# A new order for the opening of a hybrid decoder step, and other buffers for the gate's weights

## The chip, the core and the metric

The kernel runs on one core of one Trainium2 chip. A core has five engines, each with a queue of its own that it works through in order: TensorE (PE in the profile; its loads of weights are PEld) multiplies matrices and writes to PSUM; VectorE (DVE), ScalarE (ACT) and GpSimd (POOL) work element by element on SBUF, VectorE and ScalarE on PSUM too; SyncE (SP) issues DMAs here. ScalarE's queue issues DMAs as well. Engines wait for one another, and for DMAs, by semaphores.

The metric is the time of one execution on the device in microseconds (us). A profiled execution gives the trace, a time for each instruction; its span runs from the first instruction to the last.

## The reference: what is computed

One layer works on 1024 rows of a prompt and on 64 rows of samples (8 sequences of 8), each row 1024 wide, all in float32:

```python
mod = jax.nn.silu(c) @ w_ada + b_ada               # c: 1 + 8 rows, w_ada: 1024 x 3072
shift, scale, gate = jnp.split(mod, 3, axis=-1)
h = rmsnorm(x, norm_g) * (1 + scale[:, None]) + shift[:, None]
proj = h @ w_in                                    # the one large projection
u_pool, z_pool, z_ssm, xbc, dt_raw, g_raw = jnp.split(proj, SPLITS, axis=-1)
...                                                # pooling branch p, state-space branch s
gates = jax.nn.sigmoid(g_raw)
m = gates[..., :D_MODEL] * p + gates[..., D_MODEL:] * s
x = x + gate[:, None] * (m @ w_o)
```

The change lies in the first three lines and the first columns of the fourth. The gate, the last third of `mod`, isn't needed before the last line; it is computed early and put by in HBM.

## The kernel before

All 1088 rows (1024 and 64) are kept side by side as columns, so that a matrix of activations is eight tiles (k = 0 to 7) of 128 features by 1088 columns. The columns are cut into three blocks b: 0 is 256 wide, 1 is 384, 2 is 448 (384 of the prompt and the 64 samples).

**The opening** is the function `first()`. It loads x, normalises it, transposes it, computes shift and scale from `w_ada`, forms h, and does the first products with `w_in`. What it does is a set of small steps, and the order in which all engines take them is a list of words written out by hand, `ORDER1`. The steps are emitted in the order of the list, and `in_line` ties the instructions of each engine into that order (L219, the calls at the start and the end of `first`); so an engine never passes a step that waits. A word is a step's name, a number or two, and, where there is a choice, the engine: `.V` VectorE, `.A` ScalarE, `.G` GpSimd. The words that matter here:

- `sq i`: the sum of squares of 128 rows of x (VectorE L671, ScalarE L673); i = 8 is the samples. `root g`, `unit g`, `spread g`, `rsb g`: for block g the root (ScalarE), its reciprocal on a diagonal (VectorE or ScalarE), that spread over the partitions by PE (L696), and its copy to SBUF (ScalarE L705).
- `turn g.k`: PE transposes block g of x, features k, into a PSUM bank (L713): two 128-row tiles for block 0, three for 1, three and the samples for 2. `out g.k` scales it on VectorE and so frees the bank (L718). There are seven banks for all steps; a word takes the one that was freed longest ago.
- `silu`, `tab`, `cturn`, `sct`: c through SiLU, a table load for ScalarE, c transposed, and copied.
- `ada p.k`: PE multiplies c with rows k and k + 1 of part p of `w_ada` (L763). `mr`, `end`, `md` finish part p (ScalarE, PE, VectorE L778 and L781). Part p gives shift and scale for features 2p and 2p + 1.
- `h b.k`: ScalarE writes h rounded to the matmul's type (L794, L796). `ta`, `t b.k`: the same unrounded on ScalarE or VectorE (L803, L805, L812); `l b.k`: their difference, the low part (L658, a step with two inputs in SBUF). Each float32 product is made of three: high by high, low by high, high by low.
- `hi`, `lo`: the same split of a raw weight tile (L829, L658). `pr b.k`: PE adds feature tile k of block b to the first two output tiles (L844); `sg b.t` is their sigmoid and store (L857). `dt i`, `dto i`: the dt columns (L868).
- `gt k`: PE multiplies c with rows k and k + 1 of the gate's third of `w_ada` (L882); `ge` adds the bias and stores the gate.
- `ca`, `cb`, `cc`, `ce`, `s n h k`, `s n l k`: sums and differences of h for a product by seven half-sized products (Strassen's scheme), and their high and low parts (VectorE L658, ScalarE L940). S2 and S3 are two sets of four each. `wh n`, `wl n`: the same for the weights. `m n.s`: one half of the n-th of the seven products, twelve matmuls (PE L989). `u`, `z` put the products together.
- `warm n`: n matmuls whose result is not used.

**Loads.** SP's loads stand in a list `waiting`; behind each word, those at its head go out whose conditions have been said. The order is: x 0 to 4, the eight rows of part 0 of `w_ada`, two weight tiles, x 5 to 7, part 1, part 2, two more weight tiles, part 3, the dt columns, two column tiles `col`, six small loads, and the first four gate rows (`gate_load`, L606). The samples' x goes out on ScalarE's queue, behind four small loads of biases and gains. A completion semaphore is used again by a later DMA, so that an issue can wait for the landing of an earlier one.

**Buffers.** x lies in two large tiles, `xbig`, with the tag Y, of which there are two buffers; S2 and S3 later take the same two. Gate rows take three buffers with the tag R and the one with the tag sq; rows 4 to 7 take them again, and `gt` itself issues these loads, when rows k and k + 1 have been multiplied (end of `gt`).

**Behind the opening** come the units, pairs of column tiles of `w_in`, each seven half-sized products with all preparation of weights beside them (`pair`, L413 on PE, L151 and L154 for the split of weights). A planner of the language sets the order of their instructions, and PE goes from one to the next.

Of the kernel before, what the change touches and what calls it, by code (L numbers as in the profile page):

```python
# [46 lines left out]
def tile_pool_ssd_step(  # L47
# [34 lines left out]
    hs = open_("hs", 3)  # L82
# [3 lines left out]
    tfp = right.__enter__()  # L86
# [23 lines left out]
    load = nc.sync.dma_start  # L110
    store_ = nc.scalar.dma_start
# [70 lines left out]
    def x_load(i, start=None):
        n = P if i < 8 else NS
        xt = R([P, D]) if i == 8 else xbig[i // 4][:, i % 4, :D]
        (start or load)(xt[:n], x_prompt[0, i * P:(i + 1) * P, :] if i < 8 else x_sample.rearrange("b t d -> (b t) d"))
        xr[i] = (xt, n)
# [9 lines left out]
    def ada_load(part, k):  # L196
        a, b = PARTS[part]
        w = (b - a) * P
        if part == 0:
            if k == 0:  # L200
                wtile[0] = Y4(hp, F32)
            t = wtile[0][:, k // 2, k % 2 * 512:k % 2 * 512 + 2 * w]
        else:
            if k % 2 == 0:
                wtile[part, k // 2] = G((P, D))
            t = wtile[part, k // 2][:, k % 2 * 512:k % 2 * 512 + 2 * w]
        wraw[part, k] = t.rearrange("p (s c) -> p s c", s=2)
        load(wraw[part, k], w_ada[0, k * P:(k + 1) * P, 0:2 * D].rearrange("p (s c) -> p s c", s=2)[:, :, a * P:b * P])
# [49 lines left out]
    def dram(name, shape, dt=F32):  # L258
        return dr.tile(list(shape), dt, tag=name, name=name)
# [339 lines left out]


    gate_d = dram("gate_d", [NB + 1, D])
    gw, gp2 = {}, []

    def gate_load(k):
        gw[k] = hs.tile([P, D], F32, tag="sq", name=nm("gk"), bufs=1) if k % 4 == 3 else R((P, D))
        load(gw[k], w_ada[0, k * P:(k + 1) * P, 2 * D:])  # L606

    def gate_bias():
        bg = tfp.tile([P, 256], F32, tag="bg", name="bg", bufs=1)
        nc.gpsimd.memset(bg, 0.0)  # L610
        for j in range(4):
            load(bg[32 * j:32 * j + NB + 1], b_ada[0, 2 * D + 256 * j:2 * D + 256 * j + 256].partition_broadcast(NB + 1))
        return bg

    ORDER1 = """
        warm6 sq0.A silu sq1.V turn0.0 turn0.6 turn0.7 turn0.5 turn0.2 cturn tab sq2.V vturn warm2 sct root0
        sq8.V sq3.A turn0.1 warm8 unit0.V sq4.A vt spread0 root1 rsb0.A ada0.0 unit1.V ada0.2 out0.0 out0.1
        spread1 out0.2 turn1.2 out0.5 rsb1.A turn1.5 out0.6 turn1.1 out1.2 turn1.0 turn1.3 out1.1 turn1.4
        out1.3 ada0.4 out1.0 hi0.0 ada0.6 out1.5 mr0 turn0.4 hi1.0 lo0.0.V end0 turn0.3 md0 turn1.6 lo1.0.G
        turn1.7 sq5.A warm10 out0.3 out0.7 out1.4 h0.0 sq6.V h0.1 h1.0 turn2.4 t0.0.V sq7.A turn2.1 t1.0.V  # L620
        turn2.2 l0.0.V turn2.0 h1.1 l1.0.V ada1.0 t0.1.V root2 warm2 unit2.A l0.1.V ada1.2 t1.1.V warm4
        out1.6 l1.1.V ada1.4 out1.7 spread2 out0.4 pr1.0 rsb2.A out2.1 ada1.6 out2.2 mr1 turn2.7 ta2.1.A
        out2.4 end1 pr1.1 out2.0 t2.1 ta2.0.A ada2.0 md1 h2.1 ada2.2 ada2.4 t2.0 h0.3 turn2.6 h0.2 ta2.2.V
        ada2.6 h2.0 t2.2 turn2.3 mr2 hi0.1 turn2.5 l2.0.V end2 h1.3 l2.1.G out2.3 warm4 h2.2 out2.6 t1.3.A
        l2.2.V ada3.0 h1.2 l1.3.V pr2.0 hi1.1 lo0.1.G out2.7 t1.2.A md2 pr2.1 ta2.3.A l1.2.V h0.5 ta2.4.V
        ada3.2 h1.5 t2.3 ada3.4 t0.2.A ada3.6 t2.4 h2.3 pr0.0 mr3 l0.2.V h2.4 l2.3.V pr2.2 h1.4 l2.4.V h0.4
        t1.4.V pr2.3 t1.5.A t0.4.V t0.5.A l0.4.V pr0.1 l1.4.V t0.3.A lo1.1.V pr0.2 l1.5.V pr1.2 l0.5.V
        l0.3.V pr2.4 out2.5 tc.V ta2.5.A pr0.3 tb.V end3 t2.5 pr0.4 md3 pr0.5 h2.5 pr1.3 l2.5.V h1.6 ta2.6.V
        h1.7 pr2.5 ta2.7.V h0.6 t1.7.V h0.7 pr1.4 t0.6.V t1.6.A t2.6 wh0 pr1.5 l1.7.V h2.6 l0.6.V wh1 t2.7
        pr0.6 t0.7.A wl1.V gt0 h2.7 l0.7.V gt2 wl0.V gt4 l1.6.V pr0.7 l2.6.V pr1.6 sgt ca2.V pr2.6 l2.7.V  # L630
        sg0.1 ca0.V m0.0 sg0.0 cb2.V ca1.V s3h2 ca3.V pr2.7 cb1.V u0.0 m0.1 cb3.V sg2.1 cc2.V s3h3 cc3.V
        m1.0 wh4 cb0.V s2h3 s3l3.V s2h2 pr1.7 cc0.V s3h0 s2l3.V wh3 dt2 s2l2.V s2h0 d21.V sg1.1 s2l0.V wh2
        wl3.V s3h1 dt1 wl2.V sg2.0 wl4.V sg1.0 s3l2.V lx u0.1 s3l1.V dto2 gt6 cc1.V m1.1 dto1 d12.V ge s2h1
        s3l0.V lt wh5 m2.0 s2l1.V s1h3 u1.0 s1h2 s1l3.V m2.1 s1h1 s1l2.V s1h0 s1l1.V z1.0 u1.1 m3.0 s1l0.V
        wh6 wl5.V z1.1 wl6.V m3.1 u2.0 ce1.V u2.1 ce0.V s4h1 m4.0 ce3.V s4h0 ce2.V s4h3 s4l1.V m4.1 s4h2
        u3.0 s4l2.V s4l0.G u4.0 m5.0 u3.1 lc s4l3.V m5.1 u4.1 u5.0 m6.0 u5.1 z5.0 m6.1 u6.0 z5.1 u6.1 dt0
        dto0
    """.split()

    def first():  # L640
# [236 lines left out]
        def gt(k0):  # L877
            if k0 == 0:
                gp2.append(PC())
            for k in (k0, k0 + 1):  # L880
                for j in range(4):
                    mm(gp2[0][32 * j:32 * j + 32, :256], scT[:, k, :], gw[k][:, 256 * j:256 * j + 256],  # L882
                       start=(k == 0), stop=(k == KT - 1))
# [145 lines left out]
        bg = tfp.tile([P, 256], F32, tag="bg", name="bg", bufs=1)  # L1029
# [17 lines left out]
        waiting += [((), lambda: dtw.append(dt_w()))]  # L1047
        waiting += [(("end1",) + tuple(f"sq{i}" for i in range(9)), lambda: col(0)), (("end2",), lambda: col(1))]
        waiting += [((), lambda: late.append(late_loads())), ((), bg_load)]
        waiting += [(("cturn", "spread2") + tuple(f"turn2.{k}" for k in range(KT)), lambda k=k: gate_load(k)) for k in range(3)]  # L1050
        waiting += [(tuple(f"out2.{k}" for k in range(KT)), lambda: gate_load(3))]
        x_load(8, store_)

        def loads():
            while waiting and said.issuperset(waiting[0][0]):
# [3 lines left out]
                     sct=sct, vturn=vturn, vt=vt, warm=warm, ada=ada, mr=mr, end=end, md=md_, h=h, ta=scaled, t=t_, l=l,  # L1059
# [877 lines left out]
    for c in range(9):  # L1937
        n = min(P, T - c * P)
# [5 lines left out]
    for c in range(9):  # L1944
        n = min(P, T - c * P)
# [328 lines left out]
```

## Time and profile before

| | |
|---|---|
| median of 3 runs | 1267.26 us (1265.69 to 1270.69) |
| profiled execution | 1269.22 us |
| its span | 1267.5 us |
| PE busy | 1243.8 us (98%) |
| VectorE, ScalarE, GpSimd busy | 974.5, 680.9, 719.5 us |
| the opening: from the start to the first L413 on PE | 102.61 us |
| DMA in the first 110 us | 25.28 MB |

A row of the timeline gives the start and the duration in us, the engine, the line, the operation, the output and the inputs by the program's names, their size, and how many instructions of the kind are merged; in brackets stands how long the engine had been idle and what ended that. A row of the stretches gives the busy time of each engine in a window, with the number of instructions, and then the clock that TensorE was granted, the share of the DMA engines' time and GB/s. Names such as Y, R, G and gk are tags of buffers: `Y<-in_x_prompt` is a load of x, `R<-in_w_ada` and `gk<-in_w_ada` are loads of gate rows, and `pc<-R,scT` is a product with one.

### The profile page before, as it was taken

Reading aid. Unit: us, or ns where it says so; the run is one execution under the profiler, and the core shown is the slowest. Engines: PE = TensorE matmul, PEld = TensorE weight load, DVE = VectorE, ACT = ScalarE, POOL = GpSimd, SP = SyncE. Lnnn points to the kernel's source line nnn. Section 1 sums busy time; section 2 is a strip of 40 time slices with the busy share of each in tenths; the row PEclk is TensorE's granted clock in tenths of the full one; section 3 lists DMA queues with packets and bytes.
Section 4 is the critical chain, followed back from the end, with each engine's and each line's share of the span. In section 5 each row is a group of like instructions: output and inputs, shape, how many; then the busy total and the mean of one; then the engine's idle time right before and its main releaser. Section 6 shows DMA issues by size and latency. Waiting matters only on the chain.

```text
span 1267.5 us, 26537 instructions
## 1 busy us (share of the span) xinstructions
PE 1243.8 (98%) x9721; PEld 1161.0 (92%) x9721; DVE 974.5 (77%) x1719; ACT 680.9 (54%) x1565; POOL 719.5 (57%) x610
## 2 busy tenths in 40 slices
PE   8999999999999999999999999999999999999997
PEld 6779999999999999999999989998898888999886
DVE  5875689986998688876766775488687898759986
ACT  5664347465556547455656554656676655401425
POOL 1006767786868667664445434345586777503662
PEclk9999999999999999999999999999999999999999
DMA  9855444564546445444656564998888977866884
GB/s 326 247 161 191 137 157 156 179 209 154 163 151 204 153 156 185 129 143 124 184 169 198 157 191 147 328 311 269 250 252 269 294 231 247 280 214 222 246 196 158
DMA packets 264675, 257.99 MB, mean 204 GB/s; under 512 B 29889, under 2 KB 204561, under 8 KB 264538
## 3 DMA queue, kind: packets, MB, share of 16 engines
q1 hardware_dynamic: 183728, 163.66, 42.6%
q10 hardware_dynamic: 78514, 88.44, 20.3%
q0 software_dynamic: 2304, 4.20, 1.9%
q8 instruction: 77, 1.26, 0.4%
q14 instruction: 52, 0.43, 0.1%
HBM read 171.26 MB, written 85.10 MB: 202 GB/s over the span
## 4 chain that ended last, share of the span: by engine, by line
PE 64%; DVE 3%; DMA 3%; issue 1%; POOL 1%; ACT 1%; SPq 0%; ACTq 0%; DVEq 0%; POOLq 0%
PE mm L238 16%; PE mm L413 14%; PE ps L413 14%; PE ps L1265 2%; PE pc L413 2%; PE pc L1587 2%; PE ps L1268 2%; PE ps L2069 2%; PE ps L2071 2%; PE ps L2070 2%; PE ps L1355 1%; PE ps L1562 1%; PE ps L1378 1%; DMA out<-xb 1%; PE pc L1369 1%
## 5 line engine op out<-in xcount | busy, mean ns | idle before, releaser
L154 POOL TENSOR_TENSOR wlo<-rawA,whi 128x512 fp32r<-128x512 f32 x120 | 176.4, 1475 | 155.0 <-ACT whi L151 141.7
L154 POOL TENSOR_TENSOR wlo<-raw,whi 128x512 fp32r<-128x512 f32 x90 | 149.5, 1670 | 86.0 <-ACT whi L151 76.7
L238 PE MATMUL mm<-Y,whi 128*128 128x352 f32 (+1 forms) x960 | 197.4, 335 | 0.3 <-DVE Y L1625 0.3
L238 PEld LDWEIGHTS mm<-Y,whi 128*128 128x128 f32 x960 | 160.2, 189 | 6.6 <-issue 4.6
L1108 DVE SCALAR_TENSOR_TENSOR GA<-GA,cvT,GA 128x1112 f32<-128x1112 f32 x72 | 133.7, 1861 | 0.1
L413 PE MATMUL mm<-Y,whi 128*128 128x272 f32 x800 | 120.3, 292 | 0.0
L413 PE MATMUL ps<-Y,whi 128*128 128x272 f32 x800 | 117.9, 289 | 0.0
L151 ACT ACTIVATE whi<-rawA 128x512 fp32r<-128x512 f32 x120 | 75.3, 628 | 76.8 <-PE ps L413 42.4
L151 ACT ACTIVATE whi<-raw 128x512 fp32r<-128x512 f32 x90 | 55.8, 628 | 111.3 <-DVE raw L367 48.5
L413 PEld LDWEIGHTS mm<-Y,whi 128*128 128x128 f32 x800 | 107.9, 188 | 2.7 <-issue 0.9
L413 PEld LDWEIGHTS ps<-Y,whi 128*128 128x128 f32 x800 | 106.6, 188 | 0.8 <-issue 0.4
L1253 ACT ACTIVATE dec<-dec,acT 128x128 f32<-128x128 f32 (+1 forms) x288 | 86.9, 383 | 26.4 <-POOL dec L1244 25.2
L238 PE MATMUL mm<-Y,wlo 128*128 128x352 f32 (+1 forms) x480 | 99.2, 328 | 0.0
L238 PEld LDWEIGHTS mm<-Y,wlo 128*128 128x128 f32 x480 | 82.2, 189 | 0.0
L305 POOL TENSOR_TENSOR pw<-pw,ph 128x512 fp32r<-128x512 f32 x40 | 68.0, 1699 | 16.5 <-ACT ph L303 16.2
L413 PE MATMUL mm<-G,whi 128*128 128x272 f32 x480 | 71.1, 289 | 0.0
L413 PE MATMUL ps<-G,whi 128*128 128x272 f32 x480 | 70.2, 288 | 0.0
L413 PE MATMUL mm<-Y,wlo 128*128 128x272 f32 x400 | 66.7, 288 | 0.0
L413 PE MATMUL ps<-Y,wlo 128*128 128x272 f32 x400 | 66.5, 288 | 0.0
L413 PEld LDWEIGHTS mm<-G,whi 128*128 128x128 f32 x480 | 64.5, 189 | 0.7
L413 PEld LDWEIGHTS ps<-G,whi 128*128 128x128 f32 x480 | 64.2, 188 | 0.0
L1524 POOL TENSOR_TENSOR Y<-xb,Y 128x512 fp32r<-128x512 f32 x32 | 41.6, 1302 | 37.3 <-ACT Y L1522 37.3
(601 smaller groups left out, 3254.8 us busy)
## 6 DMA issues: line engine op xcount, KB each, us to landing
rawA<-in_w_in SPq DMA_DIRECT2D x62, 512.0 KB
dec<-acs_d SPq DMA_DIRECT2D x32, 512.0 KB
xbc<-GA ACTq DMA_DIRECT2D x24, 512.0 KB
Y<-wo SPq DMA_DIRECT2D x10, 1024.0 KB
pw<-in_w_ssm_out ACTq DMA_DIRECT2D x32, 256.0 KB
ws<-ph ACTq DMA_DIRECT2D x32, 256.0 KB
ws<-pw ACTq DMA_DIRECT2D x32, 256.0 KB
h<-in_state_ssm SPq DMA_DIRECT2D x32, 256.0 KB
```

What stands on the lines that cost most here:

```text
L151: ins = act(hi[:, :, :ncols], raw[:, :, :ncols], AF.Copy)
L154: (eng or nc.gpsimd).tensor_tensor(lo[:, :, :ncols], raw[:, :, :ncols], hi[:, :, :ncols].bitcast(F32), ALU.subtract)
L238: mm(ps[:, :n], w[k // 4][h][:, k % 4, :], r[k][:, o:o + n], start=(j == 0), stop=(j == len(terms) - 1))
L305: nc.gpsimd.tensor_tensor(raw.bitcast(F32R), raw, hi.bitcast(F32), ALU.subtract)
L413: mm(p, w[j // 8][:, k], A(k, s)[j // 4 == 1], start=(j == 0), stop=(j == 11))
L1108: V.scalar_tensor_tensor(d[:, :n], rp[:, k:k + n], cvT[:, 24 * k + mc:24 * k + mc + 1], d[:, :n], ALU.mult, ALU.add)
L1253: act(dec[:, h], dec[:, h], AF.Exp, bias=acT[:S, c, 8 * g + h:8 * g + h + 1], scale=-1.0)
L1265: mm(o[hh], xd[:S, 2 * q + hh, :], dec[:S, 2 * q + hh], start=True, stop=state is None)
L1268: mm(o[hh], state[:, h * 64:h * 64 + 64], cE[:, h], start=False, stop=True)
L1524: nc.gpsimd.tensor_tensor(yl[g][:, :, o:o + S], v, yhc.bitcast(F32), ALU.subtract)
L1587: mm(pu, bt, xw.rearrange("p h d -> p (h d)"), start=True, stop=True)
L2069: mm(ps, hi, y[:, k, c0:c0 + cw], start=(first and k == 0), stop=False)
```

## The change

The list `ORDER1` is replaced by another one. It has the same steps, but for the number of matmuls in `warm`; 35 of them carry another engine's letter. The loads of x go out first, all eight; the samples' x goes out on ScalarE's queue ahead of the small loads. The gate's eight rows take the two Y buffers, four rows each, and all are in SP's list behind the small loads; `gt` issues no loads any more. A function that nobody called, `gate_bias`, is deleted.

```diff
+    xs_ = R([P, D])
+    store_(xs_[:NS], x_sample.rearrange("b t d -> (b t) d"))
     vb = sm.tile([44, P], F32, tag="stc", name="vb", bufs=4)
     store_(vb[0:16, :], b_ada[0, 0:2048].rearrange("(m p) -> m p", p=P))
...
-    xr = {}
+    xr = {8: (xs_, NS)}
...
     def gate_load(k):
-        gw[k] = hs.tile([P, D], F32, tag="sq", name=nm("gk"), bufs=1) if k % 4 == 3 else R((P, D))
+        if k % 4 == 0:
+            gy.append(Y4(hs, F32))
+        gw[k] = gy[-1][:, k % 4, :D]
         load(gw[k], w_ada[0, k * P:(k + 1) * P, 2 * D:])
...
-        warm6 sq0.A silu sq1.V turn0.0 turn0.6 turn0.7 turn0.5 turn0.2 cturn tab sq2.V vturn warm2 sct root0
-        sq8.V sq3.A turn0.1 warm8 unit0.V sq4.A vt spread0 root1 rsb0.A ada0.0 unit1.V ada0.2 out0.0 out0.1
...
+        warm6 sq0.V silu sq1.V turn0.7 tab turn0.5 turn0.3 cturn turn0.2 root0 turn0.6 turn0.0 unit0.V warm2
+        sct sq8.A spread0 warm3 rsb0.A sq2.A vturn out0.7 turn0.1 warm6 sq3.V out0.1 sq4.A vt turn1.4 out0.5
+        turn1.5 out0.2 turn1.2 root1 sq5.V turn1.7 unit1.A warm4 out0.6 out0.3 spread1 out0.0 turn1.0 sq7.V
+        rsb1.A turn2.7 sq6.A turn2.6 warm1 out1.2 ada0.0 out1.4 root2 unit2.A turn2.0 out1.0 turn2.5 out1.5
+        turn2.3 out1.7 spread2 turn2.4 rsb2.A ada0.2 out2.7 ada0.4 out2.0 ada0.6 out2.3 mr0 turn2.2 out2.4
+        hi0.0 end0 out2.2 turn2.1 lo0.0.G hi1.0 turn1.6 md0 turn1.3 turn0.4 turn1.1 lo1.0.V h0.0 ada1.0 h1.0
+        ta2.0.V warm3 out1.1 t1.0.A t2.0 h1.1 ada1.2 t0.0.V warm4 h0.1 l1.0.G out2.1 h2.0 out1.6 ta2.1.A
+        ada1.4 l2.0.V t0.1.A pr1.0 t2.1 t1.1.A l0.1.G out1.3 h2.1 ada1.6 out0.4 mr1 pr2.0 l2.1.V l0.0.V
+        l1.1.G out2.5 end1 out2.6 pr2.1 md1 pr0.0 ta2.2.V ta2.3.A t2.2 pr1.1 h1.2 t2.3 h0.3 pr0.1 h2.2
...
+        t1.7.A l1.6.V ta2.6.A wl0.V pr0.7 l1.7.V ta2.7.A m0.0 d12.V sgt t2.7 pr1.6 wl1.V sg0.0 t2.6 u0.0
+        m0.1 sg0.1 ca0.V h2.6 d21.V s1h0 lt l2.6.V m1.0 u0.1 s1l0.V h2.7 wh4 l2.7.V pr2.6 wl4.V ca2.V m1.1
+        ca3.V s1h2 cb2.V s1h3 cc2.V pr2.7 wh5 ce2.V s1l3.V pr1.7 sg2.1 cb3.G lc sg2.0 gt0 dt2 s1l2.V sg1.1
+        cc3.V wh2 ce3.V sg1.0 wl2.V wh3 cb0.V gt2 dto2 wl3.V dt0 cc0.V s2h2 s2h0 s2l2.V gt4 dto0 s2l0.V dt1
+        cb1.G u1.0 s2h3 u1.1 z1.0 z1.1 cc1.V gt6 s2l3.V s4h3 m2.0 ge s3h2 s4l3.V s3h3 s3l2.V s2h1 m2.1
+        s3l3.V s3h0 s2l1.V s3h1 dto1 s3l1.V m3.0 s3l0.V s4h2 ce1.V u2.0 u2.1 s4l2.V m3.1 s4h1 u3.0 wh6
+        s4l1.V ce0.G m4.0 u3.1 wl5.G s4h0 m4.1 u4.0 s4l0.V wl6.G m5.0 u4.1 m5.1 u5.0 z5.0 m6.0 u5.1 z5.1
+        m6.1 u6.0 u6.1
...
                        start=(k == 0), stop=(k == KT - 1))
-            for k in (k0 + 4, k0 + 5):
-                if k < KT:
-                    gate_load(k)
...
-        for what in ("x04", "p0", "w", "x57", "p1", "p2"):
+        for what in ("x07", "p0", "w", "p1", "p2"):
...
-        waiting += [(("cturn", "spread2") + tuple(f"turn2.{k}" for k in range(KT)), lambda k=k: gate_load(k)) for k in range(3)]
-        waiting += [(tuple(f"out2.{k}" for k in range(KT)), lambda: gate_load(3))]
-        x_load(8, store_)
+        waiting += [(tuple(f"turn2.{k}" for k in range(KT)), lambda k=k: gate_load(k)) for k in range(KT)]
```

More of the change, by code (lines that the diff above doesn't have):

```diff
@@ L180, in tile_pool_ssd_step, with x_load @@
     hl_ = [None] * KT
[L182 to L186, printed above, removed]
+    def x_load(i):
+        xt = xbig[i // 4][:, i % 4, :D]
+        load(xt, x_prompt[0, i * P:(i + 1) * P, :])
+        xr[i] = (xt, P)
     tf = [None] * KT
@@ L601, in tile_pool_ssd_step @@
     gate_d = dram("gate_d", [NB + 1, D])
-    gw, gp2 = {}, []
+    gw, gp2, gy = {}, [], []
     def gate_load(k):
-        gw[k] = hs.tile([P, D], F32, tag="sq", name=nm("gk"), bufs=1) if k % 4 == 3 else R((P, D))
+        if k % 4 == 0:
+            gy.append(Y4(hs, F32))
+        gw[k] = gy[-1][:, k % 4, :D]
         load(gw[k], w_ada[0, k * P:(k + 1) * P, 2 * D:])
[L608 to L613, printed above, removed]
@@ L615, in tile_pool_ssd_step @@
-    ORDER1 = """
-        warm6 sq0.A silu sq1.V turn0.0 turn0.6 turn0.7 turn0.5 turn0.2 cturn tab sq2.V vturn warm2 sct root0
-        sq8.V sq3.A turn0.1 warm8 unit0.V sq4.A vt spread0 root1 rsb0.A ada0.0 unit1.V ada0.2 out0.0 out0.1
[L618 to L637, printed above, removed]
@@ new lines, in tile_pool_ssd_step @@
+    ORDER1 = """
+        warm6 sq0.V silu sq1.V turn0.7 tab turn0.5 turn0.3 cturn turn0.2 root0 turn0.6 turn0.0 unit0.V warm2
[7 more added lines that the diff above has]
+        l1.1.G out2.5 end1 out2.6 pr2.1 md1 pr0.0 ta2.2.V ta2.3.A t2.2 pr1.1 h1.2 t2.3 h0.3 pr0.1 h2.2
+        t0.3.V h2.3 ada2.0 l2.2.V h0.2 ada2.2 l2.3.V hi0.1 ada2.4 t0.2.V h1.3 lo0.1.V ada2.6 hi1.1 t1.3.V
+        pr2.2 mr2 l0.2.V t1.2.A lo1.1.V end2 l1.3.V pr2.3 l0.3.G md2 ta2.5.V pr0.2 h1.4 ta2.4.V t1.4.A t2.5
+        ada3.0 h0.4 ada3.2 t2.4 h1.5 ada3.4 t0.4.V t1.5.A ada3.6 l1.2.V h2.4 pr0.3 l1.5.V mr3 l2.4.V pr1.2
+        h2.5 h0.5 l0.4.V l1.4.V end3 t0.5.A pr0.4 l0.5.V pr1.3 l2.5.G md3 pr0.5 h0.7 tc.V t0.7.A pr2.4 h1.7
+        l0.7.V wh0 ca1.V pr1.4 h0.6 tb.V h1.6 t0.6.V pr2.5 s1h1 l0.6.V wh1 s1l1.V pr0.6 t1.6.A lx pr1.5
+        t1.7.A l1.6.V ta2.6.A wl0.V pr0.7 l1.7.V ta2.7.A m0.0 d12.V sgt t2.7 pr1.6 wl1.V sg0.0 t2.6 u0.0
[6 more added lines that the diff above has]
+        m6.1 u6.0 u6.1
```

## The prediction

> **What bounds the kernel now.** I read the page first, then the stretches of 20 us, then the timeline of the opening, where the change lies.
>
> ```profile
> span 1267.5 us, 26537 instructions
> PE 1243.8 (98%) x9721; PEld 1161.0 (92%) x9721; DVE 974.5 (77%) x1719; ACT 680.9 (54%) x1565; POOL 719.5 (57%) x610
> ```
>
> ```profile
> 20.00:40.00 20.00, 17.97 (x221) 12.95 (x211) 16.17 (x40) 12.47 (x28) 3.51 (x3) 0.91 1.09 350
> 40.00:60.00 20.00, 19.60 (x179) 17.79 (x179) 17.43 (x47) 16.23 (x30) 0.31 (x1) 1.00 0.71 215
> 60.00:80.00 20.00, 16.77 (x138) 12.38 (x134) 12.46 (x20) 7.93 (x16) 0.00 (x0) 0.91 0.44 153
> 100.00:120.00 20.00, 20.00 (x177) 18.93 (x176) 7.59 (x17) 8.70 (x18) 11.96 (x10) 1.00 0.63 204
> ```
>
> The columns of a stretch are its length, the busy time of PE, PEld, DVE, ACT and POOL, PE's clock, the DMA share and GB/s. TensorE (PE) is busy 98% of the span and all of 100 to 120, where the opening's list has given over to the units. What the opening loses or gains goes one to one into the end. The opening has the holes: in 60 to 80 PE is 3.2 us short of full, and its clock is 0.91 of full speed. PE's timeline shows where.
>
> ```profile
> 31.52 0.45 PE L844 MATMUL mm<-Y,whi 128*128 128x384 f32 x1
> ...
> 59.27 1.50 PE L882 MATMUL pc<-R,scT 128*32 128x256 f32 x24
> 60.59 0.61 PE L882 MATMUL pc<-gk,scT 128*32 128x256 f32 x8
> 63.81 0.64 PE L882 MATMUL pc<-R,scT 128*32 128x256 f32 x8 [2.61 <-DMA R<-in_w_ada]
> 65.07 1.08 PE L882 MATMUL pc<-R,scT 128*32 128x256 f32 x8 [0.62 <-DMA R<-in_w_ada]
> 66.08 0.58 PE L844 MATMUL mm<-G,whi 128*128 128x256 f32 x1
> ...
> 88.64 1.16 PE L989 MATMUL mm<-Y,whi 128*128 128x272 f32 x8
> 100.74 1.07 PE L868 MATMUL ps<-Y,dtw 128*32 128x256 f32 x16
> 102.61 1.27 PE L413 MATMUL ps<-Y,whi 128*128 128x272 f32 x8
> ```
>
> ```profile
> 64.00:66.00 2.00, 1.38 (x16) 0.20 (x8) 2.00 (x4) 0.00 (x0) 0.00 (x0) 0.71 1.04 422
> 66.00:68.00 2.00, 2.00 (x12) 1.92 (x9) 1.53 (x3) 0.23 (x1) 0.00 (x0) 0.50 0.55 197
> ```
>
> Four marks carry what follows: pr1.0 starts at 31.52, gt0 at 59.27, m3.0 at 88.64, and at 102.61 L413 takes over. Between the first two PE has hardly a hole. Behind gt2 it has one: gt4 needs rows 4 and 5 of the gate, and SP could issue their loads only when gt0 and gt2 had been read:
>
> ```profile
> SPq L606 <- PE pc L882: 7.2, 2, 6.9
> ```
>
> **The change, part by part.** Durations are those of the one profiled execution (1269.22 us, span 1267.5). The median of the three runs, 1267.26, is 1.96 below it; the sum is put on the median.
>
> *Gate rows in the buffers of x.* All eight loads now wait for the last transposes of x alone and go out one behind the other, behind col(1) and the small loads in SP's queue. col(1) waits for end2, which comes at about 42 by the walk below; with the six small loads that is 49 to 50 for the first row.
>
> ```profile
> R<-in_w_ada SPq DMA_DIRECT2D x6, 512.0 KB
> ```
>
> Eight of these at the 350 GB/s of 20 to 40 are 4.19 / 0.35 = 12 us: landed by 62. The new list puts gt0 behind the last pr, at about 70, so 8 us cover them. The two waits go, 2.61 + 0.62 us, and the half clock behind them: 0.71 in 64 to 66 and 0.50 in 66 to 68 say that PE worked from 65.07 to about 68.2 at half speed, 1.6 us lost. Together **-4.8**. Behind the same buffers stand S2 and S3 now: S2 is written after gt2, S3 after gt6; both are in the walk.
>
> *Work moved ahead of pr1.0.* Behind pr1.0 both lists have the same PE words (24 pr, 14 m, 3 dt, 4 gt, ada1.6 to ada3.6), except that four turn2 words and a warm4 stand ahead of it now.
>
> ```profile
> 11.78 2.83 PE L753 MATMUL pc<-ones 128*128 128x128 f32 x16
> 25.19 0.55 PE L713 MATMUL ps<-ident,Y 128*128 128x128 f32 x3
> 25.67 0.27 PE L713 MATMUL ps<-ident,R 64*128 64x64 f32 x1
> 25.87 0.55 PE L713 MATMUL ps<-ident,Y 128*128 128x128 f32 x3
> ```
>
> A turn2 takes 25.87 - 25.19 = 0.68, a matmul of warm 2.83 / 16 = 0.18: 4 x 0.68 + 4 x 0.18 = **-3.4**. dt0 goes from the end to the middle, which changes nothing for PE.
>
> *When pr1.0 can start.* The next rows are the timeline of the fill, and two of a later place for the price of ScalarE's steps.
>
> ```profile
> 8.03 1.04 ACT L722 ACTIVATE R<-R 9x1024 f32<-9x1024 f32 x1
> 12.95 1.22 DVE L671 SCALAR_TENSOR_TENSOR sqj<-R 64x1024 f32<-64x1024 f32 x1 [2.53 <-DMA R<-in_x_sample]
> 16.10 0.43 DVE L718 TENSOR_TENSOR tf<-ps,rsb 128x256 f32<-128x256 f32 x1 [0.22 <-ACT rsb L705]
> 18.09 1.67 DVE L718 TENSOR_TENSOR tf<-ps,rsb 128x384 f32<-128x384 f32 x3 [0.24 <-ACT rsb L705]
> 18.76 0.63 ACT L829 ACTIVATE whi<-raw 128x512 fp32r<-128x512 f32 x1 [0.71 <-DMA raw<-in_w_in]
> 21.45 1.27 POOL L658 TENSOR_TENSOR wlo<-raw,whi 128x512 fp32r<-128x512 f32 x1 [18.08 <-ACT whi L829]
> 21.48 1.27 DVE L781 TENSOR_TENSOR md<-md,vT 128x18 f32<-128x18 f32 x1
> 32.20 1.69 DVE L718 TENSOR_TENSOR tf<-ps,rsb 128x448 f32<-128x448 f32 x3 [2.68 <-ACT rsb L705]
> ...
> 85.97 1.74 ACT L940 ACTIVATE R<-tf 128x544 fp32r<-128x544 f32 x3
> 87.72 1.28 ACT L998 ACT_TABLE_LOAD   x1
> ```
>
> x5 to x7 (1.5 MB, 4.3 us at 350 GB/s) now come before w_ada's first part. The load right behind that part was in use at 18.76, so ada0.6 had its rows by 18.7 at the latest and has them at 23 now. The sample's x came with 12.95; third on ScalarE's queue I put it at 6.3, since silu at 8.03, behind a sq of 1.05 that waited for the queue, says that the small load there had gone by about 6.9.
>
> ScalarE then runs silu 6.9 to 7.95, a table load and its first use to 9.5, root0 to 9.8. unit0 on VectorE, spread0 on PE and rsb0 follow, 2 us, as from the end of the row at 12.95 to 16.10 before: first out at 11.9, against 16.10. VectorE has from there to md0 seven out0 (0.34 start to start), five out1 (0.53), five out2 (0.56), three sq (1.3 with the read) and 0.7 of small ones: 12.4, so 24.3. It runs dry before rsb1 and before root2 (0.5 each) and before rsb2 (1.7: sq6, root2, four steps of unit2 and eight matmuls of spread2 end at 24.2): 27.0. ada0.6 at 23 is not what is late, then. md0's second step falls behind lo0.0.G, as at 21.45 and 21.48, where a step of 18 elements took 1.27: 28.6. h0.0, h1.0 and t1.0 on ScalarE (three of 0.6) and l1.0.G (1.27) end at 31.9, pr1.0 starts at 32.1: **+0.6**. The bounds are 30 (no dry queue, no stretched step) and 35.5 (the sample's x at 9.7, halfway to where it was). I take 32.1, which is nearest to the row.
>
> *Steps on other engines.* 35 words carry another letter; GpSimd has eleven of them now instead of four. The pair at 21.45 shows the price: VectorE's step with two inputs in SBUF stands still while GpSimd runs. It is there the other way round too:
>
> ```profile
> 91.24 2.62 DVE L658 TENSOR_TENSOR tf<-tf,tf 128x544 f32<-128x544 f32 x4
> 92.80 2.86 POOL L154 TENSOR_TENSOR wlo<-rawA,whi 128x512 fp32r<-128x512 f32 x1 [52.49 <-ACT whi L151]
> ```
>
> GpSimd's 1.27 became 2.86 beside a train of such steps (0.65 apiece). For each step that left it VectorE saves 0.45 to 0.65 and waits between nothing, if its next step reads PSUM as out does, and 1.27. With the queue in order I get 0.5 behind l1.1.G, 0.4 behind l0.3.G, 1.3 behind l2.5.G, and 1.0 and 0.6 behind cb3.G and cb1.G: 3.8 us, less than the 4 that leave.
>
> *PE against VectorE and ScalarE behind pr1.0.* PE's words follow one another from 32.1; VectorE is at l2.0 then, 32.9, and needs 0.43, 0.45 and 0.61 for an l of block 0, 1, 2. Word by word, PE waits for l2.1 1.1, for the bank that out2.6 frees 0.4, for l1.2 and l0.4 0.3 each, and behind md3 for l0.6 and wl0 0.5. The last pr ends at 69.8. Up to m2.1 then come four gt (1.1 each by 60.59), three dt (1.9 each 256 columns by 100.74 to 102.61, 7.5 for the 1088) and two m: 84.7. S3 starts after gt6, at 81.7; ScalarE's five halves at 0.6 and VectorE's s2l1 end at 84.8, when m3.0 is due, and its table load of 1.28 falls before that. From m3.0 to the end are eight m, as from 88.64 to 100.74: 12.1, so 96.9, and 0.6 for the gaps of issue. New waits **+2.5** in all, bounds 0 (nothing late) and 7.5 (second rival).
>
> Sum: -4.8 - 3.4 + 0.6 + 2.5 = **-5.1**: the opening ends at 97.5, the span is 1262.4, the median 1262.2.
>
> **The rivals.**
> 1. The list fits: VectorE is never late, pr1.0 at 31.5: -4.8 - 3.4 = -8.2, 1259.1. For it: 4 us of steps leave VectorE. Against it: VectorE was busy 17.4 of 20 us in 40 to 60, with one GpSimd step beside it.
> 2. GpSimd holds VectorE: if each of seven steps ahead of s2l1 (l0.1, l1.1, l0.3, l2.5, cb3, cb1, ce0) costs it the whole 1.27, that is 8.9 in place of 3.8, m3.0 comes 5.1 later, and the time is 1267.3: no change. For it: 21.48 paid 1.1 of it. Against: out steps read PSUM, and those in the rows kept their time. The Trainium skill has the rule, in "SBUF — State Buffer", Who interferes with whom: a VectorE step with two inputs in SBUF and a GpSimd step that reads SBUF exclude each other for the whole instruction. The trace agrees with it at 21.48 (1.27).
> 3. The gate rows are late (slower): S2 and S3 stand behind them now. 4.19 MB from 49.5 on must land by gt6 at 80.6, and do so down to 0.13 MB/us. At 0.10 gt6 comes at 91.4, 10.8 later, and the time is 1273.0; at 0.095 it would be 1275. Against it: SP has nothing else to load in that time, and 64 to 66 shows 422 GB/s for just these rows; for it, 153 GB/s as the mean of 60 to 80.
> 4. The rows of the gate still come late because the loads ahead of them do, and the stall only moves: -4.8 falls away, 1267. It needs col(1) 12 us later than 42; I count it with rival 2.
>
> **How the numbers follow.** Forecast (1259.5 to 1265.5) 0.52, rival 1 0.19, rivals 2 and 4 0.19, rival 3 0.04; 0.06 is left for units behind the opening that the planner lays out otherwise, of either sign and mostly slower. What a measurement can tell from no change is about 0.5%, 6.3 us. Under 1260.9 are rival 1 and a fifth of the forecast: 0.30. Over 1273.6 are half of rival 3 and most of the 0.06: 0.07. Within are 0.63. The range leaves out the better half of rival 1 and all of rival 3: 1257 to 1269.
>
> **What would show it.** Right: no wait of L882 on a DMA and no clock of 0.5 behind 60 us; pr1.0 between 31 and 33; 2 to 3 us of PE at L844 and L989 that VectorE ends; L413 first at about 97.5. Wrong: two-input steps of 1.2 us and more on VectorE in many rows (rival 2); PE at half clock in 12 to 31 us because it starves in the fill; rows of L606 that land behind 70; holes of PE behind L413 that weren't there.

## The result and the profile after

The change made the kernel slower: 22 runs of each have medians of 1273.66 us (1269.45 to 1279.72) after and 1269.12 us (1265.22 to 1273.91) before, a ratio of 1.0038 with a 95% interval of 1.0026 to 1.0051, so +4.8 us (+3.3 to +6.5). The profiled execution took 1276.04 us, 2.4 above its median. Its page and its stretches of 20 us (columns as in the prediction):

```profile
span 1274.3 us, 26561 instructions
PE 1245.2 (98%) x9733; PEld 1163.7 (91%) x9733; DVE 976.5 (77%) x1709; ACT 682.1 (54%) x1568; POOL 729.6 (57%) x617
```

```profile
20.00:40.00 20.00, 19.29 (x216) 14.38 (x215) 15.85 (x37) 11.59 (x26) 3.98 (x4) 1.00 1.11 338
...
60.00:80.00 20.00, 19.50 (x195) 14.69 (x197) 17.63 (x30) 12.35 (x23) 3.58 (x2) 1.00 0.40 135
80.00:100.00 20.00, 15.33 (x122) 12.79 (x111) 15.22 (x24) 11.18 (x20) 7.83 (x5) 0.83 0.32 97
```

The hole of 60 to 80 is filled: 19.50 of 20 us at full clock. A new one, larger than the old, stands in 80 to 100: TensorE works 15.33 us there, at a clock of 0.83. TensorE's timeline shows it (start, length, line, shapes, and in brackets the idle time ahead with what ended it):

```profile
33.74 0.45 PE L840 MATMUL ps<-Y,whi 128*128 128x384 f32 x1
...
72.49 1.07 PE L878 MATMUL pc<-Y,scT 128*32 128x256 f32 x16
...
86.49 0.29 PE L982 MATMUL ps<-Y,whi 128*128 128x272 f32 x1
88.97 0.77 PE L982 MATMUL ps<-Y,whi 128*128 128x272 f32 x4 [2.19 <-ACT Y L933]
92.22 1.05 PE L982 MATMUL ps<-Y,whi 128*128 128x272 f32 x3 [2.48 <-DVE Y L654]
93.97 2.02 PE L982 MATMUL mm<-Y,whi 128*128 128x272 f32 x8
...
106.32 1.18 PE L414 MATMUL ps<-Y,whi 128*128 128x272 f32 x8
```

pr1.0 (L840 now) starts at 33.74, gt0 (L878) at 72.49, and no gt waits for a row. m3.0 starts at 86.49, does one matmul, waits 2.19 us for ScalarE's high half of S2, does four, and waits 2.48 us for VectorE's s2l1. Behind that the clock is at half: eight matmuls take 2.02 us at 93.97, where eight at full clock take 1.16 (experiment 1). The units take over at 106.32, against 102.61.

What held s2l1 is in VectorE's queue, with GpSimd's and SP's beside it:

```profile
71.14 3.57 DVE L654 TENSOR_TENSOR tf<-tf,tf 128x544 f32<-128x544 f32 x2
...
80.04 2.51 DVE L654 TENSOR_TENSOR Y<-tf,Y 128x544 fp32r<-128x544 f32 x2
84.36 0.69 DVE L368 TENSOR_TENSOR raw<-rawA 128x512 f32<-128x512 f32 x1 [1.81 <-DMA rawA<-in_w_in]
84.97 0.43 DVE L1000 TENSOR_TENSOR c<-s,mm 128x272 f32<-128x272 f32 x1
...
86.30 0.69 DVE L368 TENSOR_TENSOR raw<-raw,rawA 128x512 f32<-128x512 f32 x1
86.90 0.69 DVE L368 TENSOR_TENSOR rawA<-rawA,rawA 128x512 f32<-128x512 f32 x1
87.50 1.79 DVE L654 TENSOR_TENSOR Y<-tf,Y 128x544 fp32r<-128x544 f32 x1
...
89.55 3.88 DVE L654 TENSOR_TENSOR Y<-tf,Y 128x544 fp32r<-128x544 f32 x6
```

```profile
70.55 3.58 POOL L654 TENSOR_TENSOR tf<-tf 128x544 f32<-128x544 f32 x2 [17.24 <-DVE tf L654]
80.20 1.76 POOL L654 TENSOR_TENSOR tf<-tf,tf 128x544 f32<-128x544 f32 x1 [6.08 <-DVE tf L654]
87.12 1.59 POOL L368 TENSOR_TENSOR raw<-raw,rawA 128x512 f32<-128x512 f32 x1 [3.43 <-DVE raw L368]
```

```profile
75.14 3.54 SPq L357 DMA_DIRECT2D rawA<-in_w_in  x2
```

L368 is no word of the list. It is the weight sums of the first unit behind the opening, which the planner puts where it sees room. In the kernel before, the same sums (L367 there) came behind the list:

```profile
101.57 0.68 DVE L367 TENSOR_TENSOR raw<-rawA 128x512 f32<-128x512 f32 x1
```

Now three of them stand inside it, ahead of s2l1. The first waits 1.81 us for rows that SP asked for at 75 and 78, and u1.0 and u1.1 (L1000) stand behind it, and ScalarE's z1 and high halves behind those. A fourth, on GpSimd at 87.12, stands beside a step of VectorE that takes 1.79 us. SP asked for them that early because the list now frees the buffers of w_in earlier (the second load followed a wlo of 77.57 that read its buffer); in the kernel before they were asked for here:

```profile
82.65 1.28 SPq L356 DMA_DIRECT2D rawA<-in_w_in  x2
```

That the planner moved the sums for this reason is inferred from the order of the queues; that they stand there is seen.

### The profile page after: what moved, and what is told of

Its sections match the earlier page's. It is cut to its first block, busy times and chain, and to the rows that moved or that the text cites. A ratio compares the mean times of both kernels' runs of the same rounds, so it can differ in the third digit from the quotient of the medians.

```text
span 1274.3 us, 26561 instructions
## 1 busy us (share of the span) xinstructions
PE 1245.2 (98%) x9733; PEld 1163.7 (91%) x9733; DVE 976.5 (77%) x1709; ACT 682.1 (54%) x1568; POOL 729.6 (57%) x617
## 4 chain that ended last, share of the span: by engine, by line
PE 86%; DVE 4%; DMA 4%; ACT 3%; issue 2%; POOL 1%; SPq 1%; ACTq 0%; POOLq 0%; DVEq 0%
PE ps L414 22%; PE mm L414 22%; PE mm L239 16%; PE pc L414 5%; PE ps L1256 2%; PE pc L1578 2%; PE ps L2060 2%; PE ps L2062 2%; PE ps L2061 2%; PE ps L1259 2%; DMA R<-in_w_o 1%; PE ps L1346 1%; PE ps L1553 1%; PE ps L982 1%; DMA wo<-R 1%
## 5 line engine op out<-in xcount | busy, mean ns | idle before, releaser
L306 POOL TENSOR_TENSOR pw<-pw,ph 128x512 fp32r<-128x512 f32 x40 | 69.8, 1745 | 11.9 <-ACT ph L304 11.7
L414 PE MATMUL mm<-G,whi 128*128 128x272 f32 x480 | 71.1, 290 | 0.0
L414 PE MATMUL ps<-Y,wlo 128*128 128x272 f32 x400 | 66.6, 288 | 0.0
```

What stands on the lines that cost most here:

```text
L306: nc.gpsimd.tensor_tensor(raw.bitcast(F32R), raw, hi.bitcast(F32), ALU.subtract)
L414: mm(p, w[j // 8][:, k], A(k, s)[j // 4 == 1], start=(j == 0), stop=(j == 11))
```

## The experiments

Three causes could make the opening 8.8 us later than forecast. Theory A: the planner's sums hold VectorE's queue. Theory B: the list's own steps on GpSimd hold VectorE. Theory C: the samples' x, issued third, hold up the fill.

**1. The planner's sums behind the list.** The changed kernel; the first unit's weight steps are issued behind s4l1, twelve VectorE steps ahead of the list's end. Nothing else differs.

```diff
+            with behind(mybir.EngineType.DVE, 12) if not later_[0] else contextlib.nullcontext():
+                for _ in prep:
+                    pass
+            later_[0] = True
-            for _ in prep:
-                pass
```

> The changed kernel with one thing more: the three sums on VectorE (L368) and what follows them for the first unit's weights are issued behind s4l1 of the opening's list instead of where the planner put them (84.36, 86.30, 86.90 us, in the middle of the list). Theory A (these steps hold VectorE's queue): 1.81 us of waiting for the rows of w_in, three steps of 0.65 and 1.1 us of a step stretched beside GpSimd's L368 leave VectorE ahead of s2l1, 4.9 us in all. The waits of m3.0 (2.19 and 2.48) fall below 1 us together, the half clock of 91 to 98 us goes (2.6 us), the first L414 stands at 99 to 100 instead of 106.3, and the time is about 1267 against 1273.7. Theory B (GpSimd's eleven steps of the list hold VectorE): the waits of m3.0 stay at 3 us or more, L414 comes at 104 to 106, time 1272 to 1274.

Measured: 0.9996 of the kernel before (0.998 to 1.0011), 0.42% or 5.3 us better than the change. TensorE's timeline, then VectorE's:

```profile
87.79 0.77 PE L985 MATMUL ps<-Y,whi 128*128 128x272 f32 x4 [0.26 <-ACT Y L936]
88.82 0.64 PE L985 MATMUL ps<-Y,whi 128*128 128x272 f32 x3 [0.25 <-DVE Y L657]
89.80 1.16 PE L985 MATMUL mm<-Y,whi 128*128 128x272 f32 x8
...
100.31 1.18 PE L415 MATMUL ps<-Y,whi 128*128 128x272 f32 x8
```

```profile
92.75 1.44 DVE L369 TENSOR_TENSOR raw<-rawA 128x512 f32<-128x512 f32 x1
```

The waits of m3.0 fall from 4.67 to 0.51 us, the half clock is gone, and the units start at 100.31, 6.0 us earlier. 0.4 of this was there at pr1.0 already (33.37 against 33.74), ahead of anything that the edit touches; counted from pr1.0 it is 5.6. Theory A holds for most of what the forecast missed.

**2. cb3 and cb1 on VectorE again.** The changed kernel, two letters of the list.

```diff
-        ca3.V s1h2 cb2.V s1h3 cc2.V pr2.7 wh5 ce2.V s1l3.V pr1.7 sg2.1 cb3.G lc sg2.0 gt0 dt2 s1l2.V sg1.1
+        ca3.V s1h2 cb2.V s1h3 cc2.V pr2.7 wh5 ce2.V s1l3.V pr1.7 sg2.1 cb3.V lc sg2.0 gt0 dt2 s1l2.V sg1.1
...
-        cb1.G u1.0 s2h3 u1.1 z1.0 z1.1 cc1.V gt6 s2l3.V s4h3 m2.0 ge s3h2 s4l3.V s3h3 s3l2.V s2h1 m2.1
+        cb1.V u1.0 s2h3 u1.1 z1.0 z1.1 cc1.V gt6 s2l3.V s4h3 m2.0 ge s3h2 s4l3.V s3h3 s3l2.V s2h1 m2.1
```

> The changed kernel with cb3 and cb1 on VectorE again instead of GpSimd; the planner's steps stay where they are. Theory B: the two rows stretched beside GpSimd (71.14, two steps in 3.57 us, and 80.04, two in 2.51) go back to 1.36 each, 3.3 us less, and more behind them; the waits of m3.0 fall to 1 us or less, L414 at 100 to 102. Theory A: VectorE pays two steps of 0.65 itself, so 2.0 us are gained at most, and the wait for the rows of w_in at 84.4 takes part of it back since it ends with a transfer: the waits of m3.0 keep 3 us or more, L414 at 104 to 106, time 1272 to 1274.

Measured: 1.0011 (0.9993 to 1.0029), 3.4 us better than the change, though the two intervals still touch.

```profile
71.67 1.49 DVE L654 TENSOR_TENSOR tf<-tf,tf 128x544 f32<-128x544 f32 x2
...
79.13 2.51 DVE L654 TENSOR_TENSOR Y<-tf,Y 128x544 fp32r<-128x544 f32 x2
...
83.29 0.68 DVE L368 TENSOR_TENSOR raw<-rawA 128x512 f32<-128x512 f32 x1
```

```profile
88.22 0.76 PE L982 MATMUL ps<-Y,whi 128*128 128x272 f32 x4 [0.91 <-ACT Y L933]
90.81 0.64 PE L982 MATMUL ps<-Y,whi 128*128 128x272 f32 x3 [1.83 <-DVE Y L654]
```

The two steps that took 3.57 us take 1.49: in the changed kernel both cb3 and cb1 ran beside them on GpSimd (70.55, two steps). The pair at 80.04, which the expectation counted too, still takes 2.51 (79.13 here): the step of GpSimd beside it is ce0, which was not moved. The first L368 finds its rows there and does not wait. The last wait of m3.0 ends at 90.81 instead of 92.22, 1.4 us earlier, and this time the clock stayed whole, which gives the other 2.6: the units start at 102.30. That lies between the two theories, whose bounds were 102 and 104; I had ruled out more than 2.0 us for theory A because I did not count the clock. So GpSimd's two steps are a second, smaller cause, 1.4 us by themselves while the planner's sums stand in the queue (1.9 counted from pr1.0, which came at 34.27).

**3. TensorE kept busy ahead of m3.0.** Matmuls of ones in m3.0's bank, 40 and then 20.

```diff
-            p = bank(("m", i, s))[:, :SB]
+            t = bank(("m", i, s))
+            p = t[:, :SB]
+            for _ in range(40 if (i, s) == (3, 0) else 0):
+                mm(t[:, 272:272 + P], ones, ones, start=True, stop=True)
```

> The changed kernel with 40 matmuls of ones, which nobody reads, in m3.0's bank ahead of m3.0 (about 4.4 us of work at full clock), so that TensorE is busy while it would wait for VectorE; nothing else changes. If the half clock of 91 to 98 us follows from those waits: no stretch of 0.5 there, L414 at about 103.7 instead of 106.3, time about 1271. If it comes from something else: half clock again, L414 at 106 or later, time 1273 to 1274. VectorE's rows stand where they are either way.

Measured with 40: 1.0049 (1.0032 to 1.0067). They were too many: 80 passes of 9.10 us kept m3.0 until 95.15, so the time proves nothing, but the clock was whole and the units came at 107.24.

> As the run with 40 matmuls of ones ahead of m3.0, but 20 of them: each was two passes, 0.228 us, so 20 are 4.55 us, from 86.4 to 91.0, and m3.0 then needs s2l1 at about 92. If the half clock follows from the waits: clock 1.00 throughout, and from the end of the last wait to the first matmul of the units 12 us as in that run, so it stands at about 104 against 106.3, time 1271. If not: 106 or later.

Measured with 20: 1.0026 (1.001 to 1.0042), which does not stand apart from the change's 1.0038; the profile has the units at 103.48, 2.8 us earlier than after the change, and no half clock ahead of them.

```profile
86.09 4.63 PE L982 MATMUL ps<-ones 128*128 128x128 f32 x40
91.99 0.64 PE L985 MATMUL ps<-Y,whi 128*128 128x272 f32 x3 [0.64 <-DVE Y L654]
```

VectorE is as late as before the edit, but for 0.2 us (91.99 against 92.22). From there to the units it takes 11.5 us instead of 14.1: the 2.6 us are what the half clock behind the waits costs.

**4. The gate's rows alone.** The kernel before with its old list; only the eight loads go to the buffers of x, as soon as the last turn2 has read them, and gt6 stands behind gt4.

```diff
-        gw[k] = hs.tile([P, D], F32, tag="sq", name=nm("gk"), bufs=1) if k % 4 == 3 else R((P, D))
+        if k % 4 == 0:
+            gy.append(Y4(hs, F32))
+        gw[k] = gy[-1][:, k % 4, :D]
...
-        pr0.6 t0.7.A wl1.V gt0 h2.7 l0.7.V gt2 wl0.V gt4 l1.6.V pr0.7 l2.6.V pr1.6 sgt ca2.V pr2.6 l2.7.V
+        pr0.6 t0.7.A wl1.V gt0 h2.7 l0.7.V gt2 wl0.V gt4 gt6 l1.6.V pr0.7 l2.6.V pr1.6 sgt ca2.V pr2.6 l2.7.V
...
-        wl3.V s3h1 dt1 wl2.V sg2.0 wl4.V sg1.0 s3l2.V lx u0.1 s3l1.V dto2 gt6 cc1.V m1.1 dto1 d12.V ge s2h1
+        wl3.V s3h1 dt1 wl2.V sg2.0 wl4.V sg1.0 s3l2.V lx u0.1 s3l1.V dto2 cc1.V m1.1 dto1 d12.V ge s2h1
```

> The kernel before with one part of the change alone: the old list, but the gate's rows all go to the two buffers of x, loaded one behind the other, and gt6 stands right behind gt4 (S3 waits for its buffer otherwise). By the prediction's term: no wait of gt4 on a DMA and no half clock at 65 to 68, so 4.8 us less, the first L413 at about 97.8 instead of 102.6, time about 1264.3 against 1269.1. Rival (the stall only moves): another wait of 3 us or more opens ahead of m3.0, L413 at 101 to 103, time 1267 to 1270.

Measured: 0.9983 (0.9972 to 0.9995), 2.2 us faster than the kernel before (0.6 to 3.6). It is the one version here that is clearly faster than both kernels.

```profile
59.84 3.87 PE L884 MATMUL pc<-Y,scT 128*32 128x256 f32 x64
...
95.31 0.39 PE L988 MATMUL mm<-Y,whi 128*128 128x272 f32 x1 [0.91 <-DVE Y L660]
99.50 0.77 PE L413 MATMUL ps<-Y,whi 128*128 128x272 f32 x4
```

All 64 matmuls of the gate run without a hole. From pr1.0 to the units it takes 66.6 us (32.86 to 99.50) against 71.1 before. Only 0.9 of a new wait comes in its place. But the time gains less than half of the 4.8 us expected, and the interval leaves 4.8 out. The units start at 99.50 where 97.8 was expected, mostly since pr1.0 came 1.3 us later than in the first profile of before; where the rest of the time is missing stays open (last part of the next section).

**5. The samples' x last on ScalarE's queue again,** in the changed kernel.

```diff
     xs_ = R([P, D])
-    store_(xs_[:NS], x_sample.rearrange("b t d -> (b t) d"))
     vb = sm.tile([44, P], F32, tag="stc", name="vb", bufs=4)
...
     store_(vb[40:44, :], pool_scale[0].rearrange("(m p) -> m p", p=P))
+    store_(xs_[:NS], x_sample.rearrange("b t d -> (b t) d"))
```

> The changed kernel with the load of the samples' x issued last of the seven on ScalarE's queue instead of third; all else stays. Theory C (that load holds up the fill): the issue of the small load behind it waited until 9.68 us for its landing, and silu stands behind that issue on ScalarE, at 10.0 instead of 8.0. Now silu is at about 8.0, root0 at 10.4, the first VectorE step of out0 at 14.0 to 14.8 (sq8 on ScalarE waits for the samples' x until 13 and stands ahead of rsb0), and pr1.0 at 32 to 32.8 instead of 33.4 to 34.3; the first L414 is 1 us or more earlier, time 1 to 4 us below the changed kernel (the half clock ahead of m3.0 can go or stay). Rival: the fill is set by PE's own words or by the rows of x; pr1.0 stays at 33.3 or later, and the time within 1 us of the changed kernel.

Measured: 1.0031 (1.0017 to 1.0045), 0.9 us better than the change, inside both intervals. silu moved from 10.00 to 6.92 and the first out from 15.76 to 14.64:

```profile
14.64 0.43 DVE L714 TENSOR_TENSOR tf<-ps,rsb 128x256 f32<-128x256 f32 x1 [3.91 <-ACT rsb L701]
```

```profile
15.40 2.73 PE L749 MATMUL pc<-ones 128*128 128x128 f32 x12
```

But TensorE then waited 2.0 us for the first rsb and out (1.80 and 0.20, until 15.13), and twelve matmuls of warm ran at half clock behind that (2.73 us; 1.50 in experiment 1). pr1.0 stands at 33.74 as before, where 32 to 32.8 was expected. Theory C falls: the 3 us that silu lost do not reach pr1.0.

**6. All three edits of 1, 2 and 5 together.**

> The changed kernel with all three: the first unit's weight sums behind s4l1 of the list, cb3 and cb1 on VectorE, the samples' x last on ScalarE's queue. If the three causes are what the forecast missed: no wait of m3.0 over 0.5 us, no half clock behind 60 us, pr1.0 at 32 to 32.8, the first L413/L415-line matmul of the units at 98 to 99.3 (100.31 with the first edit alone), time 0.2% below the kernel before. If only the first edit matters, 100 to 100.5 and a ratio of 0.9996.

Measured: 0.9991 (0.9974 to 1.0009); pr1.0 at 34.02, waits of 0.7 and 0.3 in m3.0, the units at 100.23. That is experiment 1 again (100.31). Once the planner's sums are out of the way, GpSimd's two steps cost nothing that is seen: the causes lie on one path and do not add up.

**7. The samples' x third, alone,** in the kernel before with its old list.

```diff
+    xs_ = R([P, D])
+    store_(xs_[:NS], x_sample.rearrange("b t d -> (b t) d"))
     vb = sm.tile([44, P], F32, tag="stc", name="vb", bufs=4)
...
-        x_load(8, store_)
```

> The kernel before with the third part of the change alone: the samples' x issued third on ScalarE's queue; the old list. Theory C: silu at about 10 instead of 8.0 and cturn and sct with it, sq8 on VectorE 3 us earlier; in the old list root0 stands far behind both, so the first out comes between 1 us earlier and 1.5 us later than 16.10, pr1.0 at 31 to 33.5, the time within 2 us of the kernel before. The prediction's term (the samples' x at 6.3, the first out 4.2 us earlier) would put silu at 7 and pr1.0 at 30 or earlier.

Measured: 1.0001 (0.9986 to 1.0015). The profile has the next small load's issue at 9.54, silu at 10.89 and the first out at 20.33, 4.2 us later than before; pr1.0 at 33.84, the units at 104.27. Both the first out and pr1.0 are later than expected (17.6 and 33.5 at most).

```profile
9.54 0.25 ACTq L144 DMA_DIRECT2D vb<-in_pool_scale  x1
...
10.89 1.04 ACT L724 ACTIVATE R<-R 9x1024 f32<-9x1024 f32 x1
```

This part makes no difference to the time that 1.9 us either way would not hide.

**8. Both kernels profiled a second time.**

> The kernel before, unchanged, profiled a second time, to see how far the opening of one kernel moves from execution to execution. If the opening is steady to 0.5 us, the first L413 is at 102.1 to 103.1; if the fill wanders, as pr1.0 at 32.9 in the old list with the gate's buffers suggests, it is anywhere from 101 to 104. The time ratio is 1.000.

> The changed kernel, unchanged, profiled a second time. If what stands ahead of m3.0 belongs to the order of the queues, the two waits in m3.0 come again with 4 to 5 us, the half clock behind them as well, pr1.0 at 33.3 to 34.3 and the first L414 at 105.5 to 107. If it was chance, they are smaller by 2 us or more. The time ratio is 1.003 to 1.005.

Measured: 1.0003 (0.9988 to 1.0018) and 1.0023 (1.0004 to 1.0042). The changed kernel repeats its rows: waits of 2.11 and 2.49 in m3.0, half clock behind them, units at 105.81. The kernel before has its two waits of 2.60 and 0.62 again, but pr1.0 at 33.14 instead of 31.52 and the units at 103.63.

```profile
88.84 0.77 PE L982 MATMUL ps<-Y,whi 128*128 128x272 f32 x4 [2.11 <-ACT Y L933]
92.10 1.05 PE L982 MATMUL ps<-Y,whi 128*128 128x272 f32 x3 [2.49 <-DVE Y L654]
```

So the hole belongs to the order of the queues. The fill of the kernel before moves by 1.6 us, and its clock accounts for it. In the first profile TensorE's clock was 0.91 in 20 to 40, which makes some 3.4 us at half speed; in the second it was 0.83, 6.8 us:

```profile
20.00:40.00 20.00, 18.16 (x219) 13.41 (x215) 15.46 (x39) 10.92 (x25) 2.54 (x2) 0.83 1.09 351
```

3.4 us more at half speed cost 1.7. In the changed kernel the clock is whole there.

## Why the prediction was wrong, step by step

The forecast put the start of the units at 97.5 us; it was 106.32, 8.8 later. The misses: pr1.0 1.6 (33.74 for 32.1); pr1.0 to m3.0 0.15 (52.75 us for the 52.6 from 32.1 to 84.7); waits inside m3.0 4.67; the half clock behind them about 2.6. These make 9.0, and 0.2 came back in the last products. Besides, the kernel before stood at 1269.12 in the 22 runs, 1.9 above the median the sum was put on.

*m3.0's wait, put at nothing inside the new waits of +2.5: the step that failed.* "S3 starts after gt6, at 81.7; ... VectorE's s2l1 end at 84.8, when m3.0 is due": the work of VectorE was added up from the words of the list, as if the queue held nothing else. It held L368 as well, and s2l1 came at 92. Experiment 1 gives the price of this: 6.0 us of the opening, 5.3 in time; of it about 3.4 is VectorE's lateness (s2l1 read at 88.82 instead of 92.22) and 2.6 the half clock behind it. With the sums out of the way the stretch from pr1.0 to the units is 66.9 us, where the forecast had 65.4. What comes nearest to this case in the text is "units behind the opening that the planner lays out otherwise", with 0.06 and no price of its own.

*Gate rows: -4.8, right in kind, and nearly in size for the opening.* The rows go out from 49.32 on, as said (49 to 50), no gt waits, 60 to 80 runs at full clock. Alone (experiment 4) the part takes 4.4 us from the stretch between pr1.0 and the units of the first profile of before, 3.8 from that of the second (70.5 us); the time gains only 2.2 (0.6 to 3.6). Rivals 3 and 4 did not come: no row was late.

*Four turn2 and warm4 ahead of pr1.0: -3.4, of which 2.7 at most could be there.* The trace of the kernel before has 32 matmuls of warm, and the last starts at 14.34. They are those of warm6, warm2 and warm8, two passes for each matmul; the warm4 behind pr1.0 left none, so 0.7 of the term is nothing. (A word of warm emits nothing when too few banks are free. The row of 2.83 us is warm8, so one matmul of it is 0.35 and not 0.18.) The rest went into waits: from pr1.0 to the units the new list without the planner's sums takes 66.9 and 66.2 us (experiments 1 and 6), the old one with the gate's part 66.6 (experiment 4). TensorE waits 2.9, 2.2 and 0.9 us in these stretches; without the waits 64.0 stand against 65.7. The list saves TensorE 1.7 us there and pays them in waits.

*pr1.0 at +0.6: it came at +2.2, within the stated bounds, but not by the walk.* pr1.0 was at 33.35 to 34.27 in the kernels with the new list, 1.8 to 2.7 behind 31.52, though within 1.2 of the 33.14 of the second profile. The walk took VectorE as what sets pr1.0, with the first out at 11.9; the first out came at 15.76, 3.9 late, and pr1.0 was only 1.6 late. TensorE itself set it: from 11.1 on, when silu lets cturn go, it works without a pause until pr1.0, and matmuls of warm, whose result nobody uses, take 5.45 of 22.5 us of it. The second row counts the line of warm (L749) alone:

```profile
11.20:33.70 22.50, 22.50 (x238) 19.17 (x238) 15.32 (x40) 13.28 (x30) 1.27 (x1) 1.00 1.09 354
11.20:33.70 22.50, 5.45 (x32) 5.01 (x32) 1.00 1.09 354
```

Whether pr1.0 comes earlier with fewer of them was not tested. The samples' x at 6.3 was wrong as well: it landed by 9.7, and silu stood behind an issue that waited for it. Experiment 5 gives silu its 3 us back, and the waits and the half clock behind it take them again; experiment 7 shows no difference in time.

*pr1.0 to m3.0 within 0.15 us was luck.* The waits in this stretch were about 1.3 us instead of the 2.5 forecast, and the work was longer by about as much, since the 3.4 us were not all there.

*Rival 2 was there, and the mechanism was right:* VectorE's steps beside GpSimd took 3.57 us for two, and a single one 1.79. The Trainium skill's "SBUF — State Buffer", Who interferes with whom, has a VectorE step with two inputs in SBUF and a GpSimd step that reads SBUF exclude each other; the rows agree with it (3.57 for two beside cb3 and cb1, 1.49 without). These two words made VectorE wait 2.1 us, where the walk had 1.6. But moving them back was worth 1.4 us of itself (experiment 2), and nothing that is seen once the planner's sums stood elsewhere (experiment 6).

*Where 1 to 3 us are still open.* The prediction let the opening's loss or gain go one to one into the end. The opening was later by 3.7 and 2.2 us in the two pairs of profiles, 2.9 in the mean, and the time by 4.8 (3.3 to 6.5). The other way round, experiments 1, 4 and 6 reach the units 2.3 to 4.1 us earlier than the two profiles of the kernel before, and their times gain 0.5, 2.2 and 1.1 us. Each time 1 to 3 us are missing, about as much as the intervals leave open. From the first matmul of the units to TensorE's last it takes 1157.5, 1159.7 and 1155.9 us with the old buffers (before twice, experiment 7), 1160.0 and 1160.5 after the change, and 1156.5 to 1163.9 in the other seven profiles. One part of the spread is half clock: none to four pieces of 3.4 us fall there, each worth 1.7 (0.89 of full speed in 1125 to 1130 in the changed kernel's first profile is one). The other part is waits: TensorE is idle there for 6.4 to 7.4 us in the three profiles with the old buffers, for 8.8 and 9.5 after the change, and for 7.1 to 9.6 in the other seven. So some 2 us of the change may fall behind the opening as waits; which step causes them was not tested.

## What to carry to other kernels

A list written for an engine is not its queue: before adding up its words, look at what the planner may put between them, above all work that is set free by a buffer that the list now releases earlier. Where such work waits for a load, everything behind it in the queue waits too, so it is worth tying it behind the last urgent step. Look in the trace whether a word emits anything before you price it: here one that was worth 0.7 us on paper emitted nothing. When a hole on TensorE is moved, price the half clock behind it with it, since here it made a lateness of 3.4 us into 6.0.

## What the runs showed of the hardware

The half clock came in whole pieces of 3.4 us, here two in a row, and followed waits of 2.19 and 2.48 us with 0.77 us of work between. These stretches of 5 us of the changed kernel show it; PEclk is the third number from the end:

```profile
85.00:90.00 5.00, 2.55 (x19) 2.10 (x17) 5.00 (x9) 4.16 (x9) 1.59 (x1) 1.00 0.15 56
90.00:95.00 5.00, 2.78 (x12) 2.78 (x13) 5.00 (x10) 2.60 (x7) 0.00 (x0) 0.62 0.14 47
95.00:100.00 5.00, 5.00 (x31) 5.00 (x30) 2.12 (x5) 1.46 (x3) 2.75 (x2) 0.69 0.55 159
```

The 0.38 and 0.31 of 5 us that are missing at half speed make 3.8 and 3.1 us, together two times 3.4. In the kernel before, 0.71, 0.50 and 0.94 in the three stretches of 2 us from 64 to 70 make one piece.

The Trainium skill's "TensorE: Matmul & The Clock Gate", Part 1: The HAM clock gate, gives a window of about 3.4 us and half rate after at least one idle window. The length of the pieces agrees; that no wait here was as long as a window, and work stood between them, says that the window need not be wholly idle.

How long the waits are does not decide it alone. Waits of 0.91 and 1.83 us with 0.76 of work between left the clock whole in experiment 2; waits of 0.84 and 0.97 us in the fill of the kernel before (second profile, until 23.39 and 24.96) were followed by two pieces of half clock. Where they fall seems to count. In the traces' records of the clock its changes stand whole multiples of 3.41 us apart (91.24, 98.06 and 1128.89 in the changed kernel). Of the piece ahead of the first, 87.83 to 91.24, TensorE was idle for 2.6 us. Cut in the same way, the waits of experiment 2 fall into two pieces, 86.17 to 89.58 and 89.58 to 92.99, with 1.5 and 1.2 us idle. In the fill and at the gate's rows of the kernel before, half clock came behind pieces with less idle time too (0.9 us in the first profile's fill, 1.6 in both places of the second), so the idle share is not the whole rule either. That experiment 2 was spared the half clock is then partly luck.
